# Eight more weight tiles per layer as three products, their rests by accumulating transfers, in a two-layer hybrid trunk

## The chip, the cores and the metric

The kernel runs on one core of a Trainium2 chip. The metric is the device time of one execution in microseconds (us), the median of several runs. Five engines work side by side, each in the order of its own queue: TensorE (PE: matrix products, with PEld for its weight loads), VectorE (DVE), ScalarE (ACT), GpSimd (POOL) and SyncE (SP). SP, ACT and POOL also issue transfers, which 16 DMA engines carry.

## The reference, cut to what matters

Two layers run over 272 tokens (16 learned ones and 256 of the input) of width 1024. Each layer is a mixer (a causal convolution and an attention, both gated) followed by a sparse part (PEER) that selects 16 of 16384 experts for each of 8 heads.

```python
def _mixer_block(x, ...):
    h = _rmsnorm(x, mix_g)
    z = h @ w_in
    conv_in, c_q, c_kv, k_rope, gate_logits = (z[..., :o0], z[..., o0:o1], z[..., o1:o2],
                                              z[..., o2:o3], z[..., o3:])
    ...
    gates = jax.nn.sigmoid(gate_logits)
    merged = gates[..., :D_MODEL] * y_conv + gates[..., D_MODEL:] * y_mla
    return x + merged @ w_out

def _peer(h, wq, keys, u_table, v_table):
    q = (hf @ wq).reshape(T, PEER_HEADS, 2, PEER_HALF)
    s = jnp.einsum('thpd,hpnd->thpn', q, keys)
    sv, si = lax.top_k(s, PEER_TOPK)
    ...
        a = jnp.einsum('ted,td->te', u_table[ib], xb)
        act = jax.nn.gelu(a) * wb
        return jnp.einsum('te,ted->td', act, v_table[ib])
```

The change touches two of the products: the gate logits (2048 columns of `w_in`, that is 16 tiles of 128) and the queries `hf @ wq` (2048 columns, 16 tiles).

## The kernel before, in words

The weights stream through a ring of four buffers of 1 MB (`wraw`); each holds two tiles of 128 x 1024. `next_w` takes the next tile and issues, on SP, the load that is due; `peek_w(n)` looks at the tile n further on. A load waits until the last reader of the buffer it overwrites is done.

A **plain tile** (`ztile`) is eight products of a 128 x 128 block of float32 weights with the activations (272 columns, in the second layer 256). Each shows in the profile as two matmul records, so a plain tile shows as x16. A **three-product tile** (`three`) splits weights and activations into a high part, rounded to the type float32r, and a rest: high x high, rest x high and high x rest, 24 products, each one record. `high` writes the high part of the weights (ACT), `low` the rest (weights less high part): on DVE, on POOL, or, for the query tiles 21, 23, 25 and 27, in two steps: ACT writes the negative of the weights (L711), and an accumulating transfer that POOL issues (L717) adds the weights: the destination holds the negative of the rounded weights, and w is added.

In the tables the key `"g5"` is gate tile 5, the keys 16 to 31 are the query tiles 0 to 15 (in the query loop the index is `16 + i`), and 0 to 15 are the output tiles between them. `kinds` gives the pair of buffers that a split uses: `wq0` and `wq1`, `seln` and `upad`, `acc` and `sqa`, halves of `kh` or of `sq`, or `wq0`/`wq1` with a part of `xh`.

One layer runs in this order on PE. First the tiles for queries, keys and the conv (four pairs, c = 0 to 3). Then the loop over 16 gate tiles (L859), each followed by a step of the attention (`next(att)`: key scales, scores, transposes, mixing) and by taps of the depthwise conv (`taps`: DVE multiplies and adds; `conv2` has ACT make products `cp`, which POOL's accumulating transfers sum into `part`, L673). Gate tiles 10 to 15 (`TPG`) are three-product tiles. Then the output products, and the loop over 16 query tiles (L1156): tiles 0 to 11 by three products, 12 to 15 plain. Each query tile is evacuated by ACT (`qr`, L1172); its scores against the keys are multiplied one tile later (`scores`), and DVE finds the best 16 (`top16`). Then the stage A multiplies all tokens with the table u (128 tiles), and a stage V with the table v, beside gathers of single expert rows.

Nine loads of u are issued early, inside the query loop: `EPLACE` gives, for the iteration that issues a load, which of the list `EARLY` it is and the buffer (`sq`, `kh`, `g0`, `g1`, or one of a pool of its own, `we`). Nothing reorders the program: each engine executes its instructions in the order in which the code issues them, and waits by semaphores. SP executes its loads in order too, so a load that waits holds back those behind it.

`MIXQ` names the tiles that live to the end of the query loop (pool `mpa`); the others of the mixer are in `mpb`, which is closed when the query loop begins (L982).

## Time and profile before

| | |
|---|---|
| median of 3 runs | 1658.9 us (1658.65 to 1661.19) |
| the profiled execution | 1659.62 us, its span 1657.8 us |
| mean granted TensorE clock | 1.000 |
| data moved | 568.52 MB, mean 343 GB/s |
| transfers of SP and ACT (q1), share of 16 engines | 50.7% |
| transfers of POOL (q0), share of 16 engines | 35.0% |

The profile is one execution. A group's line gives busy time and mean length; a timeline row gives start, length, engine, source line, operation, output and inputs, shapes and count, and in brackets the idle time before it and what ended it. A wait costs something only on the engine that sets the end at that place. Lengths of neighbouring matmuls overlap, so a tile is measured here from start to start. Lines are those of the kernel before.

### The profile page before, as it was taken

The page shows a single profiled execution, that of the slowest core. Times are in us where ns is not written, and L with a number is a line of the kernel's source. Part 1 is how long each engine was busy: PE and PEld are TensorE (multiplying, and loading weights), DVE is VectorE, ACT ScalarE, POOL GpSimd, SP SyncE. Part 2 cuts the span into 40 slices and gives each one's busy share as a digit, 9 for nine tenths or more (in the row PEclk, how much of TensorE's full clock was granted, in tenths as well). Part 3 has the DMA queues.
Part 4 walks back from the last instruction along what each step waited for, and adds up shares of the span by engine and source line. Part 5 has one row for each costly group of instructions (what it writes and reads, how often), then busy time and mean ns, then how long its engine had stood idle before and what let it go on. Part 6 is the DMA issues. An engine that isn't in the chain of part 4 may idle for free.

```text
span 1657.8 us, 30712 instructions
## 1 busy us (share of the span) xinstructions
PE 1642.4 (99%) x11827; PEld 1468.5 (89%) x11827; DVE 1261.6 (76%) x3082; ACT 693.3 (42%) x1803; POOL 333.0 (20%) x347
## 2 busy tenths in 40 slices
PE   9999999999999999999999999999999999999999
PEld 7679999999999999999986899999999997566655
DVE  5799899897898544444447998897877886788885
ACT  3565733435554111000024576433445443455554
POOL 0000033221222222222200100432211222233330
PEclk9999999999999999999999999999999999999999
DMA  6444697999999999999962746989999999999994
GB/s 249 113 128 177 242 345 298 424 383 424 416 423 418 424 424 423 424 424 424 417 259 85 176 153 242 340 348 396 362 425 409 409 391 411 420 425 425 424 425 191
DMA packets 86099, 568.52 MB, mean 343 GB/s; under 512 B 10328, under 2 KB 15384, under 8 KB 18744
## 3 DMA queue, kind: packets, MB, share of 16 engines
q1 hardware_dynamic: 50608, 338.51, 50.7%
q0 software_dynamic: 34560, 227.31, 35.0%
q8 instruction: 93, 1.52, 0.4%
q10 hardware_dynamic: 784, 0.74, 0.1%
q14 instruction: 54, 0.44, 0.1%
HBM read 556.18 MB, written 1.05 MB: 336 GB/s over the span
## 4 chain that ended last, share of the span: by engine, by line
PE 87%; DMA 8%; DVE 3%; ACT 1%; issue 1%; POOL 0%; SPq 0%; DVEq 0%; ACTq 0%; POOLq 0%
PE A L62 34%; PE po L62 25%; PE z L62 20%; DMA wraw<-vt 5%; PE aps L62 5%; PE wp L62 2%; DMA X<-vt 2%; DMA sqa<-wraw 1%; DVE acc L661 1%; PE xp L62 0%; PE sc L62 0%; DVE xh L1549 0%; PE wp L1262 0%; DVE tkw L1008 0%; ACT wr L1547 0%
## 5 line engine op out<-in xcount | busy, mean ns | idle before, releaser
L62 PE MATMUL A<-xh,wraw 128*128 128x160 f32 x3520 | 498.0, 300 | 0.0
L62 PEld LDWEIGHTS A<-xh,wraw 128*128 128x128 f32 x3520 | 481.1, 190 | 0.0
L62 PE MATMUL z<-xg,wraw 128*128 128x272 f32 (+2 forms) x832 | 194.1, 392 | 0.0
L1440 DVE SCALAR_TENSOR_TENSOR g<-g,xr 128x1024 f32<-128x1024 f32 x94 | 114.8, 1221 | 90.8 <-DMA g<-uv,iww 90.8
L62 PEld LDWEIGHTS z<-xg,wraw 128*128 128x128 f32 (+1 forms) x832 | 151.8, 189 | 35.0 <-issue 5.8
L1415 POOL DMA_INDIRECT g<-uv,iww x94 | 113.6, 1209 | 306.3 <-DVE va L1425 197.4
L1451 ACT ACTIVATE am<-am 128x1 f32<-128x1 f32 x208 | 40.9, 196 | 312.1 <-DVE g L1440 157.8
L62 PE MATMUL po<-Xh,wraw 128*128 128x160 f32 x1040 | 143.1, 300 | 1.0 <-DMA wraw<-vt 0.9
L62 PEld LDWEIGHTS po<-Xh,wraw 128*128 128x128 f32 x1040 | 141.5, 190 | 2.0 <-DMA wraw<-vt 2.0
L62 PE MATMUL po<-X,wraw 128*128 128x160 f32 x1008 | 138.4, 299 | 1.8 <-DMA wraw<-vt 1.3
L62 PEld LDWEIGHTS po<-X,wraw 128*128 128x128 f32 x1008 | 137.1, 190 | 2.7 <-DMA wraw<-vt 1.0
L1425 DVE SCALAR_TENSOR_TENSOR va<-g,am,va 128x1024 f32<-128x1024 f32 x91 | 116.5, 1281 | 0.3 <-ACT am L1452 0.2
L1340 ACT ACTIVATE ohA<-ohE,wlo 128x128 f16<-128x128 f16 x320 | 105.3, 428 | 5.2 <-DVE ohE L1337 4.4
L1440 DVE SCALAR_TENSOR_TENSOR kh<-kh,xr 128x1024 f32<-128x1024 f32 x48 | 58.6, 1221 | 42.5 <-DMA kh<-uv,iww 42.5
L1440 DVE SCALAR_TENSOR_TENSOR sq<-sq,xr 128x1024 f32<-128x1024 f32 x48 | 58.7, 1222 | 39.4 <-DMA sq<-uv,iww 39.4
L1415 POOL DMA_INDIRECT sq<-uv,iww x48 | 58.0, 1209 | 151.1 <-DVE va L1425 90.6
L1415 POOL DMA_INDIRECT kh<-uv,iww x48 | 59.9, 1248 | 140.4 <-DVE va L1425 92.8
L661 DVE SCALAR_TENSOR_TENSOR acc<-upad,cols,acc 128x272 f32<-128x272 f32 (+1 forms) x198 | 83.0, 485 | 0.2
L1351 ACT ACTIVATE Xh<-wp 128x260 f32<-128x260 f32 (+19 forms) x80 | 24.6, 307 | 131.5 <-DVE Xh L1348 124.8
L1425 DVE SCALAR_TENSOR_TENSOR va<-sq,am,va 128x1024 f32<-128x1024 f32 x48 | 61.5, 1281 | 5.5 <-ACT am L1452 5.5
L1425 DVE SCALAR_TENSOR_TENSOR va<-kh,am,va 128x1024 f32<-128x1024 f32 x48 | 61.5, 1282 | 3.7 <-ACT am L1452 3.7
L1452 ACT ACTIVATE am<-am,iww 128x1 f32<-128x1 f32 x208 | 61.3, 295 | 6.9
(503 smaller groups left out, 3075.0 us busy)
## 6 DMA issues: line engine op xcount, KB each, us to landing
wraw<-u SPq DMA_DIRECT2D x110, 1024.0 KB, 9.2
wraw<-vt SPq DMA_DIRECT2D x109, 1024.0 KB, 12.2
wraw<-w_in SPq DMA_DIRECT2D x27, 1024.0 KB, 4.7
X<-vt SPq DMA_DIRECT2D x17, 1024.0 KB, 11.4
wraw<-wq SPq DMA_DIRECT2D x16, 1024.0 KB, 4.8
we<-u SPq DMA_DIRECT2D x10, 1024.0 KB, 12.1
wraw<-w_out SPq DMA_DIRECT2D x8, 1024.0 KB, 4.6
wraw<-w_mla SPq DMA_DIRECT2D x4, 1024.0 KB, 5.1
```

Source lines behind the costliest of these rows:

```text
L62: PE.matmul(o, l, r, start=start, stop=stop, skip_group_check=True)
L661: V.scalar_tensor_tensor(acc[:, c, t0:], u_, weight(c, k), acc[:, c, t0:], op0=OP.mult, op1=OP.add)
L1340: S.activation(A_[1][:, t // 2, :, t % 2], E[0][:, t // 2, :, t % 2], AF.Copy, scale=wlo[:, 4 * b + t:4 * b + t + 1])
L1351: S.activation(x_, p[:, :, a:b].rearrange("p t j -> p j t"), AF.Copy, scale=1.0 / WS)
L1415: G.indirect_dma_start(out=g_, out_offset=None, in_=a[f"uv{l}"], in_offset=bass.IndirectOffsetOnAxis(ap=iww[i].bitcast(I32)[:, m // 16, 0, ...
L1425: V.scalar_tensor_tensor(vac[i], r, m_, vac[i], op0=OP.mult, op1=OP.add)
L1440: V.scalar_tensor_tensor(u_, u_, 1.0, xrs[i], op0=OP.mult, op1=OP.mult, accum_out=m_)
L1451: S.activation(m_, m_, AF.Gelu_apprx_tanh)
L1452: S.activation(m_, m_, AF.Copy, scale=iww[i][:, m // 16, 1, m % 16:m % 16 + 1])
```

## The change

Gate tiles 1, 3, 5 and 7 and query tiles 12 to 15 become three-product tiles, in both layers. Their rests, like those of query tiles 5, 7, 9 and 11 before, are made by an accumulating transfer (`BYDMA`). For all twelve the order of the products changes: high x high for the whole tile, then high x rest of the activations, and the rest of the weights last. Gate tiles 1 and 5 use `wq0` and `wq1`, tiles 3 and 7 a new buffer `gp`. The splits of tiles 1 and 3 are issued after the last conv pair, that of tile 5 after gate tile 1, that of tile 7 after gate tile 3. The splits of query tiles 12 to 15 are issued in the iterations 9 to 12. Since they hold `sq` and the activations' parts in `g0` and `g1` longer, three early loads of u move: `sq` from iteration 9 to 13, `g0` and `g1` from 12 and 13 to 15. Six names that only the query loop uses go to a pool of their own, opened when `mpb` is closed.

```diff
-TPG = (10, 11, 12, 13, 14, 15)
+TPG = (1, 3, 5, 7, 10, 11, 12, 13, 14, 15)
+ONLYQ = {"tkw0", "tkw1", "tkw2", "tkm", "scs", "qm"}
...
-EPLACE = {1: (4, None), 4: (0, "kh"), 5: (5, None), 7: (6, None), 8: (7, None), 9: (1, "sq"), 11: (8, None), 12: (2, "g0"), 13: (3, "g1")}
+EPLACE = {1: (4, None), 4: (0, "kh"), 5: (5, None), 7: (6, None), 8: (7, None), 11: (8, None), 13: (1, "sq"), 15: (2, "g0"), 15.5: (3, "g1")}
+BYDMA = ("g1", "g3", "g5", "g7", 21, 23, 25, 27, 28, 29, 30, 31)
...
-        kinds = {"g10": 0, "g11": 1, "g12": "k", "g13": 0, "g14": 1, "g15": "s", 0: "k", 1: 0, 2: 1, 3: "s", 4: "k",
-                 19: "k", 20: "a", 21: "q", 22: "w", 23: "s", 24: "q", 25: "a", 26: "s", 27: "w"}
+        kinds = {"g1": "v", "g3": "p", "g5": "v", "g7": "p", "g10": 0, "g11": 1, "g12": "k", "g13": 0, "g14": 1, "g15": "s", 0: "k", 1: 0, 2: 1, 3: "s", 4: "k",
+                 19: "k", 20: "a", 21: "q", 22: "w", 23: "s", 24: "q", 25: "a", 26: "s", 27: "w", 28: "q", 29: "a", 30: "s", 31: "w"}
...
-            if x == "w":
+            if x == "p":
+                t_ = mp.tile([128, 2048], F32, name="gp")
+                hi, lo = t_[:, 0:1024], t_[:, 1024:2048]
+            elif x in ("w", "v"):
                 hi, lo = [mp.tile([128, 1024], F32, name=f"wq{y}") for y in range(2)]
...
-            if i in (21, 23, 25, 27):
+            if i in BYDMA:
                 S.activation(parts[i][1], w_, AF.Copy, scale=-1.0)
...
             hi, lo, _ = parts[i]
+            if i in BYDMA:
+                for w_, x, f, e in ((hi, xs[0], first, None), (hi, xs[1], None, None), (lo, xs[0], None, end)):
+                    for c in cs:
+                        mm(p, w_[:, c * 128:(c + 1) * 128], x[:, c, t0:], c == f, c == e)
+                return
...
             next(att, None)
+            if c == 3:
+                for k in (1, 3):
+                    high(f"g{k}", k)
+                    low(f"g{k}")
...
-            new = [f"g{i + 2}"] if i + 2 in TPG else []
+            new = [f"g{i + 2}"] if i >= 8 and i + 2 in TPG else []
...
+            if i in (1, 3):
+                high(f"g{i + 4}", 3)
+                low(f"g{i + 4}")
...
         mixb.close()
+        qo.append(mixs.enter_context(tc.tile_pool(name=f"qo{l}", bufs=1)))
...
-            for k in {0: (2, 3), 1: (5,), 2: (4,), 3: (7,), 4: (6,), 5: (9,), 6: (8,), 7: (11,), 8: (10,)}.get(i, ()):
+            for k in {0: (2, 3), 1: (5,), 2: (4,), 3: (7,), 4: (6,), 5: (9,), 6: (8,), 7: (11,), 8: (10,), 9: (12,),
+                      10: (13,), 11: (14,), 12: (15,)}.get(i, ()):
```

Three places show how the order of instructions moves. ACT before, in layer 0, from the end of the conv pairs to the evacuation of gate tile 1 (`cp` are the conv copies, `g` the gates):

```order
L670 ACTIVATE cp<-upad,cols_61 128x272 x4
L832 ACTIVATE bz<-z 128x272
L459 ACTIVATE mq<-aps 128x272
L670 ACTIVATE cp<-upad,cols_61 128x272 x4
L874 ACTIVATE g_618<-z 128x272
L670 ACTIVATE cp<-upad,cols_61 128x272
L874 ACTIVATE g_618<-z 128x272
```

The same place on ACT now:

```order
L462 ACTIVATE mq<-aps 128x272
L673 ACTIVATE cp<-upad,cols_61 128x272 x4
L715 ACTIVATE wq_618<-wraw 128x1024
L717 ACTIVATE wq_619<-wraw 128x1024
L715 ACTIVATE gp<-wraw 128x1024
L717 ACTIVATE gp<-wraw 128x1024
L889 ACTIVATE g_627<-z 128x272
L673 ACTIVATE cp<-upad,cols_61 128x272
L889 ACTIVATE g_627<-z 128x272
L715 ACTIVATE wq_686<-wraw 128x1024
L717 ACTIVATE wq_687<-wraw 128x1024
```

Four copies of gate tiles 1 and 3 stand between the conv copies and the evacuation of gate tile 0; two of tile 5 follow the evacuation of tile 1.

PE now, in layer 0, from gate tile 0 to gate tile 3 (`seln` rows are the key scales, `kh,xh` rows the scores):

```order
L64 MATMUL z<-xg,wraw 128x272 x8
L64 MATMUL aps<-mq,seln 128x272 x4
L64 MATMUL z<-uk,wq_618 128x272 x8
L64 MATMUL z<-un,wq_618 128x272 x8
L64 MATMUL z<-uk,wq_619 128x272 x8
L64 MATMUL aps<-mq,seln 128x272 x4
L64 MATMUL aps<-kh,xh 128x144
```

Before, one plain tile (`z<-xg,wraw`, x8) stood in the place of the three rows between the key scales; now the rest of the weights (`wq_619`) is read by the last eight of 24 products, one plain tile and four small products after gate tile 0 began.

SP before, in layer 0, at the end of the query loop (`iww` is the spread of the selected indices, which waits for DVE):

```order
L1170 DMA sq<-u 128x2048
L95 DMA wraw<-u 128x2048
L1170 DMA we_2619<-u 128x2048
L95 DMA wraw<-u 128x2048
L1170 DMA g_2669<-u 128x2048
L1170 DMA g_2717<-u 128x2048
L95 DMA wraw<-u 128x2048
L1150 DMA iww_1975<-ew 128x1x64
```

The same place on SP now:

```order
L97 DMA wraw<-u 128x2048
L1191 DMA we_2716<-u 128x2048
L97 DMA wraw<-u 128x2048
L1191 DMA sq<-u 128x2048
L97 DMA wraw<-u 128x2048
L1169 DMA iww_2060<-ew 128x1x64
L1191 DMA g_2939<-u 128x2048
L1191 DMA g_2941<-u 128x2048
```

The load into `sq` stands behind two ring loads and one early load that it preceded, the loads into `g0` and `g1` behind a ring load and the spread of the indices.

More of the change, by code (lines that the diff above doesn't have):

```diff
@@ L34 @@
 EARLY = (0, 1, 2, 3, 8, 10, 12, 14, 16)
-EPLACE = {1: (4, None), 4: (0, "kh"), 5: (5, None), 7: (6, None), 8: (7, None), 9: (1, "sq"), 11: (8, None), 12: (2, "g0"), 13: (3, "g1")}
+EPLACE = {1: (4, None), 4: (0, "kh"), 5: (5, None), 7: (6, None), 8: (7, None), 11: (8, None), 13: (1, "sq"), 15: (2, "g0"), 15.5: (3, "g1")}
+BYDMA = ("g1", "g3", "g5", "g7", 21, 23, 25, 27, 28, 29, 30, 31)
 JS = 63
-MIXQ = {"xg", "uk", "qr", "rq_w", "rq_x", "rq_ym", "tkw0", "tkw1", "tkw2", "tkm", "sk", "scs", "qm",
+MIXQ = {"xg", "uk", "qr", "rq_w", "rq_x", "rq_ym", "sk",
         "wq0", "wq1", "seln", "upad", "acc", "sqa", "g0", "g1"}
@@ L230, in trunk_kernel @@
         mixb = ExitStack()
+        qo = []
         mpa = mixs.enter_context(tc.tile_pool(name=f"mixq{l}", bufs=1))
@@ L237, in tile @@
             def tile(shape, dt, name, **kw):
-                return (tw if name in ("sq", "kh", "g0", "g1") else mpa if name in MIXQ else mpb).tile(shape, dt, name=name, **kw)
+                return (tw if name in ("sq", "kh", "g0", "g1") else qo[0] if name in ONLYQ else mpa if name in MIXQ else mpb).tile(shape, dt, name=name, **kw)
         zs = ExitStack()
@@ L715, in low @@
             hi, lo, w_ = parts[i]
-            if i in (21, 23, 25, 27):
+            if i in BYDMA:
                 G.dma_start(lo, w_, accum_op=OP.add)
@@ L723, in three @@
             hi, lo, _ = parts[i]
+            if i in BYDMA:
+                for w_, x, f, e in ((hi, xs[0], first, None), (hi, xs[1], None, None), (lo, xs[0], None, end)):
+                    for c in cs:
+                        mm(p, w_[:, c * 128:(c + 1) * 128], x[:, c, t0:], c == f, c == e)
+                return
             for c in cs:
@@ L1162, in trunk_kernel @@
                 z = ztile(t0)
-            for k in {0: (2, 3), 1: (5,), 2: (4,), 3: (7,), 4: (6,), 5: (9,), 6: (8,), 7: (11,), 8: (10,)}.get(i, ()):
+            for k in {0: (2, 3), 1: (5,), 2: (4,), 3: (7,), 4: (6,), 5: (9,), 6: (8,), 7: (11,), 8: (10,), 9: (12,),
+                      10: (13,), 11: (14,), 12: (15,)}.get(i, ()):
                 high(16 + k, k - i - 1)
                 low(16 + k)
-            if i in EPLACE:
-                k, n = early_[l][EPLACE[i][0]], EPLACE[i][1]
-                raws[k] = (two(n).rearrange("p (a b) -> p a b", a=2) if n else
-                           ep.tile([128, 2, 1024], F32, name=f"we{i}"))
-                nc.sync.dma_start(raws[k], srcs[k])
+            for e in (i, i + 0.5):
+                if e in EPLACE:
+                    k, n = early_[l][EPLACE[e][0]], EPLACE[e][1]
+                    raws[k] = (two(n).rearrange("p (a b) -> p a b", a=2) if n else
+                               ep.tile([128, 2, 1024], F32, name=f"we{i}"))
+                    nc.sync.dma_start(raws[k], srcs[k])
             qT_ = mp.tile([128, T], F32, name="qr", bufs=2)
```

## The prediction, made before the changed kernel ran

> **What bounds the kernel now.** The first part of the page gives each engine's busy time, share of the span and instruction count. The fourth gives the chain that ended last.
>
> ```profile
> PE 1642.4 (99%) x11827; PEld 1468.5 (89%) x11827; DVE 1261.6 (76%) x3082; ACT 693.3 (42%) x1803; POOL 333.0 (20%) x347
> ...
> PE 87%; DMA 8%; DVE 3%; ACT 1%; issue 1%; POOL 0%; SPq 0%; DVEq 0%; ACTq 0%; POOLq 0%
> ```
>
> TensorE (PE) is the bound, but 99% is an average over stages. The change touches two stages per layer: the gate tiles (60 to 145 us in layer 0) and the query tiles (198 to 257 us). The view by stretches shows both; its columns are stretch, length, busy time of PE, weight loads, DVE, ACT and POOL, the granted clock, DMA share and GB/s.
>
> ```profile
> 80.00:120.00 40.00, 40.00 (x234) 31.72 (x227) 36.15 (x100) 26.51 (x76) 2.57 (x3) 1.00 0.52 146
> 200.00:240.00 40.00, 40.00 (x326) 39.05 (x325) 35.76 (x230) 19.20 (x36) 19.04 (x16) 1.00 0.93 307
> ```
>
> PE has no idle time in either, so a shorter tile pays at once and a new wait of PE costs in full. DVE is close behind at 36 of 40 us. The view of waits says how little PE waits now:
>
> ```profile
> PE z L62 <- DMA sqa<-wraw: 1.7, 1, 1.7
> ...
> PE aps L62 <- DVE zkr L747: 0.7, 1, 0.7
> ```
>
> The first row matters: in layer 1 PE already waited 1.7 us for a rest made by an accumulating transfer, the device that the change uses in twelve tiles per layer instead of four.
>
> **What a tile gains.** The timeline of PE (start, length, instruction) around one three-product tile (x24) and one plain tile (x16) of layer 0, and score starts around one of each in layer 1:
>
> ```profile
> 234.26 0.61 PE L62 MATMUL sc<-uk,qr 128*128 128x128 f32 x4
> 234.62 3.26 PE L62 MATMUL z<-g,wq 128*128 128x272 f32 x24
> 237.72 0.61 PE L62 MATMUL sc<-uk,qr 128*128 128x128 f32 x4
> 238.16 3.83 PE L62 MATMUL z<-xg,wraw 128*128 128x272 f32 x16
> 241.83 0.61 PE L62 MATMUL sc<-uk,qr 128*128 128x128 f32 x4
> ...
> 1047.12 0.61 PE L62 MATMUL sc<-uk,qr 128*128 128x128 f32 x4
> 1050.40 0.60 PE L62 MATMUL sc<-uk,qr 128*128 128x128 f32 x4
> ...
> 1072.83 0.61 PE L62 MATMUL sc<-uk,qr 128*128 128x128 f32 x4
> 1076.72 0.61 PE L62 MATMUL sc<-uk,qr 128*128 128x128 f32 x4
> ```
>
> From score to score a plain tile takes 241.83 - 237.72 = 4.11 us, a three-product tile 237.72 - 234.26 = 3.46: a gain of 0.65 us. In layer 1 (256 columns) it is 3.89 - 3.28 = 0.61. Eight tiles per layer: 8 x 0.65 + 8 x 0.61 = 10.1 us, if nothing waits.
>
> **Gate tile 1: a new wait.** Its two copies and its transfer are issued only after the conv copies of ACT at the end of the last pair, one plain tile ahead of their use. The rows of ACT and PE at that place, layer 0 and layer 1:
>
> ```profile
> 71.58 1.75 ACT L670 ACTIVATE cp<-upad,cols 128x272 f32<-128x272 f32 x4
> 75.72 3.93 PE L62 MATMUL z<-xg,wraw 128*128 128x272 f32 x16
> ...
> 911.60 1.85 ACT L670 ACTIVATE cp<-upad,cols 128x256 f32<-128x256 f32 x4
> 915.52 3.72 PE L62 MATMUL z<-xg,wraw 128*128 128x256 f32 x16
> ```
>
> The price of making a rest this way is seen at query tile 5 (21 in the tables): two copies, POOL's issue, and the landing counted from that issue (then the spread over all eight such transfers, and the quickest one of the conv's partial sums, 408 KB instead of 512).
>
> ```profile
> 199.28 1.05 ACT L709 ACTIVATE sq<-wraw 128x1024 fp32r<-128x1024 f32 x1
> 200.23 1.05 ACT L711 ACTIVATE sq<-wraw 128x1024 fp32r<-128x1024 f32 x1
> 201.81 0.86 POOL L717 DMA_DIRECT2D sq<-wraw  x1 [92.12 <-PE z L62]
> ...
> DMA to landing us min/median/max: 6.2/6.2/6.2
> ...
> DMA to landing us min/median/max: 6.2/9.1/12.6
> ...
> DMA to landing us min/median/max: 4.1/4.1/4.1
> ```
>
> So: conv copies end at 73.33, two copies take 0.95 + 1.05 = 2.0, POOL starts 0.53 later: issued at 75.86. With the undisturbed 6.2 us the rest lands at 82.1. The changed tile runs its 16 products with the high part first, 16/24 of 3.10 us, so PE reaches the rest at 75.72 + 2.07 = 77.8 and **waits 4.3 us**. Layer 1: issued at 911.60 + 1.85 + 2.0 + 0.53 = 915.98, landed at 922.2, needed at 915.52 + 1.93 = 917.45: **4.7 us**. Queued behind it on PE are the key scales, all scores and every later gate tile, and DVE waits for those. I take 6.2 because weights are nearly loaded there; by 4.1 the waits are 2.2 and 2.6, by 12.6 they are 10.7 and 11.1. Below nothing they can't be: even the quickest landing misses by 2 us.
>
> [...]
>
> Tiles 3, 5 and 7 are issued two tiles or more ahead, some 10 us, and wait for nothing at 6.2. The eight copies on ACT (8.4 us) lie in its idle time before the first softmax; the evacuation of tile 0 comes 4 us later, covered by three buffers. Without that cover it would cost PE those 4 us. POOL's later conv transfers queue behind the rests but are wanted only at 118 us.
>
> Gates: 4.3 - 4 x 0.65 = +1.7 in layer 0, 4.7 - 4 x 0.61 = +2.3 in layer 1. DVE is pushed back by the wait too and catches up in its own idle time:
>
> ```profile
> 112.43 1.36 DVE L492 TENSOR_REDUCE mx<-aps 128x1 f32<-128x144 f32 x4 [1.55 <-PE aps L62]
> ```
>
> That swallows 1.55 us; the rest is late at the layer norm, where PE waits already in layer 1. I add 0.3 (between 0 and 1).
>
> **The last four query tiles.** They gain 4 x 0.65 = 2.6 and 4 x 0.61 = 2.4. Their copies stand on ACT behind a wide copy that itself waits for DVE:
>
> ```profile
> 230.96 1.91 ACT L1064 ACTIVATE tx<-it 128x2048 f16<-128x2048 f16 x1 [3.71 <-DVE it L1062]
> ...
> 1060.59 1.91 ACT L1064 ACTIVATE tx<-it 128x2048 f16<-128x2048 f16 x1 [2.99 <-DVE it L1062]
> ...
> 1073.73 0.35 ACT L1083 ACTIVATE ew<-ce,rsT 128x64 f32<-128x64 f32 x1 [2.86 <-DVE ce L1082]
> ```
>
> In layer 0 the copies of the first of the four (tile 12) run from 232.8 to 234.8, so the evacuation behind them ends at 235.1 and the score that PE had at 234.26 waits 0.8. The rest is issued at 235.3, lands at 241.5 and is needed at 238.16 + 0.8 + 2.07 = 241.0: 0.5 more. With 10 us, as a neighbour's transfer had, it would be 4. The next three are ahead. Layer 0: -2.6 + 1.3 = -1.3.
>
> In layer 1 the same gives 0.9 and 0.6, and the last tile, whose copies stand behind the copy at 1073.73, about 1.0 (0.4 to 1.8). The old wait of 1.7 goes, because the rest is now used last. Layer 1: -2.4 - 1.7 + 2.5 = -1.6. Without any new wait the two layers would give -6.7.
>
> **Loads that move.** Three loads of u go later on SP, two of them behind the spread of the indices:
>
> ```profile
> 255.31 0.62 SPq L1150 DMA_DIRECT2D iww<-ew  x1
> ...
> 257.09 4.61 PE L62 MATMUL A<-xh,kh 128*128 128x160 f32 x32 [0.59 <-ACT idxT L1036]
> ...
> 266.76 8.45 PE L62 MATMUL A<-xh,g 128*128 128x160 f32 x61
> ...
> 256.00:260.00 4.00, 3.41 (x31) 3.06 (x30) 3.96 (x28) 1.01 (x4) 0.00 (x0) 1.00 0.04 8
> ```
>
> They can start at about 256 and are wanted at 265.5 and 4.5 us later. The DMA engines are idle there (0.04), so two loads of 1 MB have 9 us. I cost them at nothing; behind other traffic they took this long:
>
> ```profile
> DMA to landing us min/median/max: 14.8/15.9/16.8
> ```
>
> and then PE would wait 256 + 15.9 - 265.4 = 6.5 us per layer. The pool for query-only tiles issues nothing; its first writes come long after the last use of the memory under it: nothing.
>
> **Sum:** 1.7 + 2.3 + 0.3 - 1.3 - 1.6 = **+1.4 us**. The profiled execution took 1659.6 us (span 1657.8), so 1661.0 for it; the median of the runs is 0.7 lower: **1660.3 us**, 0.1% above before. A measurement of this kernel can tell about 0.2% (3.3 us) from no change.
>
> **Rivals.**
> - *The rests land early* (4.1 us): gates 2.2 + 2.6 - 5.0 = -0.2, queries -6.7 + 1.7 = -5.0: 1653.7. For it: less weight traffic at the gates. Against it: none of eight landed under 6.2. Chance 0.15.
> - *PE comes back slow.* [...] Its first products, at the start of the program, show the slow rate: 22 in 5.06 us is 0.23 us each, against 0.11 for a score product (0.44 for 4):
>
> ```profile
> 2.01 5.06 PE L62 MATMUL z<-ones 128*128 128x128 f32 x22 [2.01 <-DVE strip L144]
> ```
>
>   Half of 5 us is lost, 2.5 per layer: 1665.3. It decides only if the wait is long enough; no later wait in this trace passes 2 us, so no row shows the threshold. Chance 0.12. [...]
> - *The rests queue behind weights* (9.1 us, the median above): 2.9 more at tile 1 and at the first of the four query tiles, in both layers: +11.6, 1671.9. For it: seven of eight were slower than 6.2. Against it: three loads of u leave just that stretch of the query tiles. Chance 0.13.
> - *The moved loads are late*: 13 us, 1673.3. Chance 0.05.
> - *DVE is the true bound of the query stage*, and its savings don't arrive: +4.3, 1663.2. DVE is full from 228 to 256, but its last results are copied away by ACT for PE. Chance 0.07.
>
> My case holds 0.48, of which 0.43 lies within 0.2% and 0.05 above. Faster by over 0.2%: 0.15 (the first rival). Slower by over 0.2%: 0.05 + 0.12 + 0.13 + 0.05 + 0.07 = 0.42. The range from 1653.5 to 1666 leaves out the two rivals near 1672 (0.18).
>
> **What would show it.** In the trace after, PE should wait once per layer at gate tile 1 for `wq<-wraw`, 4 to 5 us; gate tiles 3, 5 and 7 not at all; the first query tile of the four under 1 us; the wait for `sqa<-wraw` in layer 1 gone; the A stage without a wait for `g<-u`. Gate wait under 2.5 us, or two waits of over 2 us among the queries, would make the prediction wrong. So would products of 0.23 us behind the wait.

## The result and the profile after

The changed kernel takes 1677.0 us (median of four runs, 1675.5 to 1678.0) beside 1659.1 us for the kernel before on the same chip: a ratio of 1.0105, interval 1.0087 to 1.0122. The change costs 18 us. 1660.3 was predicted, between 1653.5 and 1666; the measured time lies 11 us above that range. The profiled execution has a span of 1674.2 us, 16.4 more than before, and its mean granted clock is 0.993, not 1.000.

The first row of the page's part 1, and the first row of its chain, for the kernel after:

```profile
PE 1643.3 (98%) x11955; PEld 1474.3 (88%) x11955; DVE 1262.3 (75%) x3082; ACT 722.9 (43%) x1835; POOL 364.5 (22%) x363
...
PE 86%; DMA 9%; DVE 2%; issue 1%; ACT 1%; POOL 0%; DVEq 0%; SPq 0%; POOLq 0%; ACTq 0%
```

PE has almost the same busy time as before (1642.4), though eight tiles per layer should need 10 us less. So PE lost time in two ways: it stood idle 15 us more, and it was slower while busy. The view of PE's waits names the idle part (engine and tile, what it waited for: total us, times, longest):

```profile
PE z L64 <- DMA sq<-wraw: 7.8, 2, 4.4
PE z L64 <- DMA wq<-wraw: 7.6, 3, 3.3
...
PE sc L64 <- ACT qr L1193: 1.2, 2, 0.7
...
PE aps L64 <- DVE zkr L758: 0.7, 1, 0.7
PE z L64 <- DMA upad<-wraw: 0.5, 1, 0.5
PE z L64 <- DMA sqa<-wraw: 0.2, 1, 0.2
```

The new rows add up to 17.3 us (7.8 + 7.6 + 1.2 + 0.5 + 0.2), less the 1.7 us of the old wait for `sqa`: 15.6. The five that matter, in PE's timeline: gate tile 1 of layer 0 with what follows it, then query tile 12 of layer 0, gate tile 1 of layer 1, query tiles 12 and 15 of layer 1. (The names show which buffer a product reads: `z<-uk,wq x8` behind `z<-un,wq` are the rest products of gate tile 1.)

```profile
75.37 1.28 PE L64 MATMUL z<-uk,wq 128*128 128x272 f32 x8
76.48 1.16 PE L64 MATMUL z<-un,wq 128*128 128x272 f32 x8
80.95 1.27 PE L64 MATMUL z<-uk,wq 128*128 128x272 f32 x8 [3.31 <-DMA wq<-wraw]
82.16 1.29 PE L64 MATMUL aps<-mq,seln 2*128 2x272 f32 x8
83.38 3.14 PE L64 MATMUL aps<-kh,xh 98*128 98x144 f32 x8
86.31 5.14 PE L64 MATMUL z<-xg,wraw 128*128 128x272 f32 x16
...
248.55 1.52 PE L64 MATMUL z<-g,sq 128*128 128x272 f32 x8 [3.45 <-DMA sq<-wraw]
...
928.25 1.78 PE L64 MATMUL z<-uk,wq 128*128 128x256 f32 x8 [2.73 <-DMA wq<-wraw]
...
1086.18 2.08 PE L64 MATMUL z<-g,sq 128*128 128x256 f32 x8 [4.38 <-DMA sq<-wraw]
...
1100.30 1.21 PE L64 MATMUL z<-g,wq 128*128 128x256 f32 x8 [1.50 <-DMA wq<-wraw]
```

Read the lengths behind the first wait: the eight products for the key scales take 1.29 us (0.74 before), the scores 3.14 (1.67), the plain tile 5.14 (3.93). The view by stretches has the reason in its clock column (stretch, length, busy time of PE, weight loads, DVE, ACT, POOL, the granted clock, DMA share, GB/s):

```profile
80.00:82.00 2.00, 1.04 (x8) 1.05 (x8) 0.00 (x0) 0.00 (x0) 0.00 (x0) 1.00 0.96 184
82.00:84.00 2.00, 2.00 (x12) 1.15 (x12) 0.54 (x2) 1.74 (x3) 0.00 (x0) 0.53 0.91 287
84.00:86.00 2.00, 2.00 (x7) 1.65 (x7) 2.00 (x6) 2.00 (x3) 1.16 (x2) 0.50 0.58 246
86.00:88.00 2.00, 2.00 (x6) 1.54 (x5) 1.97 (x8) 0.71 (x4) 0.59 (x1) 0.50 1.01 195
88.00:90.00 2.00, 2.00 (x8) 1.53 (x8) 2.00 (x6) 2.00 (x9) 0.00 (x0) 0.76 1.04 198
```

From 82 to 89 us TensorE had half its clock. What that costs is 2 us times the part missing in each row: 2 x (0.47 + 0.50 + 0.50 + 0.24) = 3.4 us, as much as the wait itself. The same sum gives 3.4 us behind the wait of gate tile 1 in layer 1 and 1.7 behind each wait of query tile 12.

To see where the 16.4 us arise, take five stretches of the program, each from one PE instruction to the next: the **gate stretch** from the first key-scale product (75.04 us before) to the first query score (201.63), the **query stretch** from there to the first product of A (257.09), the **long stretch** of both tables to the first key-scale product of layer 1 (914.85), and gate and query stretch of layer 1 (to 1034.05 and 1086.47). After, they are longer by 4.2, 3.4, 0.5, 3.7 and 5.2 us; the start and the end of the program, outside the five, are 0.8 us shorter together. Four of them agree with the parts read above: wait + clock - gain is 3.3 + 3.4 - 2.6 = 4.1 and 2.7 + 3.4 - 2.4 = 3.7 for the gates; 4.2 + 1.7 - 2.6 = 3.3 for the queries of layer 0, and 7.1 - 1.7 + 1.7 - 2.4 = 4.7 for those of layer 1, half a microsecond short. These sums are my reading; the experiments test them.

### The profile page after: what moved, and what is told of

Same layout as the page of the kernel before. It is cut to its first block, busy times and chain, and to the rows that moved or that the text cites. A ratio compares the mean times of both kernels' runs of the same rounds, so it can differ in the third digit from the quotient of the medians.

```text
span 1674.2 us, 31059 instructions
## 1 busy us (share of the span) xinstructions
PE 1643.3 (98%) x11955; PEld 1474.3 (88%) x11955; DVE 1262.3 (75%) x3082; ACT 722.9 (43%) x1835; POOL 364.5 (22%) x363
## 3 DMA queue, kind: packets, MB, share of 16 engines
q0 software_dynamic: 36864, 235.70, 37.1%
HBM read 556.18 MB, written 1.05 MB: 333 GB/s over the span
## 4 chain that ended last, share of the span: by engine, by line
PE 86%; DMA 9%; DVE 2%; issue 1%; ACT 1%; POOL 0%; DVEq 0%; SPq 0%; POOLq 0%; ACTq 0%
PE A L64 33%; PE po L64 25%; PE z L64 18%; DMA wraw<-vt 5%; PE aps L64 5%; PE wp L64 2%; DMA wq<-wraw 1%; DMA X<-vt 1%; DVE acc L664 1%; DMA sq<-wraw 1%; PE sc L64 1%; PE xp L64 0%; DVE xh L1570 0%; PE wp L1283 0%; ACT wr L1568 0%
## 5 line engine op out<-in xcount | busy, mean ns | idle before, releaser
L1436 POOL DMA_INDIRECT g<-uv,iww x94 | 123.7, 1316 | 297.6 <-DVE va L1446 196.9
L64 PE MATMUL z<-xg,wraw 128*128 128x272 f32 (+2 forms) x576 | 135.8, 398 | 0.0
L64 PEld LDWEIGHTS z<-xg,wraw 128*128 128x128 f32 (+1 forms) x576 | 105.7, 190 | 27.5 <-issue 5.1
```

Source lines behind the costliest of these rows:

```text
L64: PE.matmul(o, l, r, start=start, stop=stop, skip_group_check=True)
L1436: G.indirect_dma_start(out=g_, out_offset=None, in_=a[f"uv{l}"], in_offset=bass.IndirectOffsetOnAxis(ap=iww[i].bitcast(I32)[:, m // 16, 0, ...
```

## The experiments

Fifteen kernels. The table has what each stretch took beyond the kernel before in its profiled execution, in us, and the timed result. Each entry is one execution: pool_q_g357 and pool_q_g357_l0, whose code is the same up to the gates of layer 1, differ by 1.2 us in the long stretch. The start and the end of the program, which have no column, add between -0.9 and +2.7 us.

| kernel | gates, layer 0 | queries, layer 0 | long | gates, layer 1 | queries, layer 1 | median us | ratio to before, interval |
|---|---|---|---|---|---|---|---|
| after | +4.2 | +3.4 | +0.5 | +3.7 | +5.2 | 1677.0 | 1.0087 to 1.0122 |
| gates_only | +4.1 | -0.1 | +0.2 | +9.8 | -2.0 | 1673.0 | 1.0050 to 1.0098 |
| queries_only | 0.0 | +4.5 | 0.0 | 0.0 | +4.6 | 1668.1 | 1.0035 to 1.0068 |
| order_loads | 0.0 | -0.1 | +1.4 | 0.0 | -2.0 | 1658.1 | 0.9976 to 0.9995 |
| filled | +0.7 | +2.6 | +0.3 | +2.7 | +5.8 | 1673.1 | 1.0068 to 1.0102 |
| part_filled | +0.7 | +1.9 | +0.4 | +6.0 | +5.3 | 1675.8 | 1.0076 to 1.0120 |
| early_rests | +4.0 | +2.1 | +0.3 | +2.1 | +4.2 | 1673.7 | 1.0071 to 1.0115 |
| queries_less_load | 0.0 | +3.2 | +2.4 | +0.1 | +2.5 | 1666.5 | 1.0024 to 1.0050 |
| pool_gate1 | -0.7 | +3.4 | +2.0 | +1.0 | +5.5 | 1675.3 | 1.0082 to 1.0119 |
| pool_all | +0.9 | -2.1 | +3.8 | +5.4 | -3.2 | 1665.2 | 1.0019 to 1.0045 |
| pool_queries | 0.0 | -2.1 | +4.3 | 0.0 | -3.2 | 1658.4 | 0.9984 to 1.0002 |
| pool_q_g357 | -2.0 | -2.0 | +2.4 | +3.5 | -3.2 | 1659.5 | 0.9989 to 1.0007 |
| pool_q_g57 | -1.3 | -2.0 | +2.8 | +3.6 | -3.2 | 1660.5 | 0.9995 to 1.0013 |
| pool_q_g357_kd | -2.0 | -2.0 | +3.2 | +8.4 | -3.2 | 1664.0 | 1.0013 to 1.0031 |
| pool_q_g357_l0 | -2.0 | -2.0 | +3.6 | 0.0 | -3.2 | 1657.1 | 0.9969 to 0.9988 |
| l0_sq9 | -2.0 | -2.0 | +1.9 | 0.0 | -3.2 | 1656.6 | 0.9974 to 0.9992 |

### Which part loses it

gates_only makes the last four query tiles plain again:

```diff
-8: (10,), 9: (12,), 10: (13,), 11: (14,), 12: (15,)}.get(i, ())
+8: (10,)}.get(i, ())
```

> The changed kernel with its last four query tiles plain again; gate tiles 1, 3, 5 and 7 keep three products. Theory A (the time is lost where PE waits for a late rest, and half as much again because the granted clock then stands near 0.5 for some 6 us): gate tile 1 costs the waits of 3.3 and 2.7 us plus 3.4 us of clock in each layer, the four tiles gain 5.0, and the product order gains 1.7: 1659.1 + 6.0 + 6.8 - 5.0 - 1.7 = 1665.2. Theory B (the waits are all, and the lower clock has another cause, such as more work per us on the engines): 1659.1 + 6.0 - 5.0 - 1.7 = 1658.4 with the clock at 1.00 in the query stage and possibly at the gates. Theory C (the gates are innocent, the queries lose it all): 1653.

queries_only makes gate tiles 1, 3, 5 and 7 plain again:

```diff
-TPG = (1, 3, 5, 7, 10, 11, 12, 13, 14, 15)
+TPG = (10, 11, 12, 13, 14, 15)
-                for k in (1, 3):
+                for k in ():
-            if i in (1, 3):
+            if i in ():
```

> The changed kernel with gate tiles 1, 3, 5 and 7 plain again; the last four query tiles keep three products. Theory A: new waits of 4.2 us in layer 0 and 7.1 in layer 1, 3.5 us of clock, less 5.0 for the tiles and 1.7 for the old wait: 1659.1 + 8.1 = 1667.2. Theory B (the waits alone): 1663.7. If the gates lose it all: 1653 or less.

order_loads has both edits.

> What is left of the change without any new three-product tile: rest products last in query tiles 5, 7, 9 and 11, three loads of u later, query-only tiles in their own pool. Theory A: the old wait for sqa in layer 1 goes, nothing else: 1659.1 - 1.7 = 1657.4. Rival (the moved loads or the pool cost something by themselves): 1659 or more, with PE waiting for g in the stage after the query tiles.

Measured: 1673.0, 1668.1 and 1658.1. Both parts lose, and what is left without them is 0.1% faster than before (0.9976 to 0.9995): 2.0 us are gained in the query stretch of layer 1, where the old wait for `sqa` is gone, and 1.4 us lost in the long stretch. queries_only came out as theory A said; order_loads is near its 1657.4, though the loss in the long stretch was not in that theory. gates_only did not: its gate stretch in layer 1 is 9.8 us longer, not 3.7. The wait for the rest is 3.6 us there, and a second one has come, at the layer norm, which theory A did not have. PE's waits in gates_only, and then DVE's from 905 to 1000 us:

```profile
PE aps L64 <- DVE zkr L758: 3.6, 1, 3.6
```

```profile
DVE acc L682 <- DMA part<-cp: 2.9, 1, 2.9
```

PE waits for DVE's sum `zkr`, and DVE has waited for the conv's last partial sum, which a transfer of POOL's queue adds up. That is the same queue in which the rests now stand. This is taken up below.

### Is it the idle time that halves the clock?

filled gives PE more work: products whose sums are thrown away, ahead of the real ones, of about the length of the wait.

```diff
+FILL = {'g1': (25, 21), 28: (27, 36)}
...
             if i in BYDMA:
+                for y in range(FILL[i][l] if i in FILL else 0):
+                    mm(p, hi[:, y % 8 * 128:y % 8 * 128 + 128], xs[0][:, y % 8, t0:], True, True)
                 for w_, x, f, e in ((hi, xs[0], first, None), (hi, xs[1], None, None), (lo, xs[0], None, end)):
```

> The changed kernel with more work: ahead of the real products of gate tile 1 and query tile 12, PE runs 25 and 27 (layer 0), 21 and 36 (layer 1) extra products, whose sums are thrown away, so that it arrives at the rest about when the rest lands. Theory A (the clock halves because PE stood idle): the rests come as late as before, the waits shrink to under 1 us, the granted clock stays at 1.00 there, and the time falls by the 10 us of clock: 1677 - 10.3 = 1666.7. Theory B (the clock falls for another reason): no gain, 1677 or more, with the clock still at 0.5 behind both places.

part_filled is the same with `{'g1': (10, 14), 28: (15, 16)}`.

> The changed kernel with fewer extra products ahead of gate tile 1 (10 in layer 0, 14 in layer 1) and query tile 12 (15 and 16), so that waits of about 2.0, 1.0, 1.5 and 2.5 us remain. If the clock falls after any wait, it falls after all four. If it takes an idle window as long as the shortest wait that was followed by a fall so far (2.7 us), the granted clock stays at 1.00 behind all four and the time is near 1673, as with all waits filled. If the threshold lies between, the windows behind each wait show where.

The mean clock of filled is 1.000 in the profiled execution (0.997 to 1.000 in all four), and with more work the kernel is no slower but rather faster: its span is 5.1 us shorter than that of the kernel after, its median 3.9 (the intervals of the two ratios overlap). At gate tile 1 of layer 0 the reading is exact. PE's timeline of filled there, the same place as above, and then the rest products of query tiles 13, 14 and 15 of layer 1:

```profile
75.34 4.41 PE L65 MATMUL z<-uk,wq 128*128 128x272 f32 x33
79.58 1.16 PE L65 MATMUL z<-un,wq 128*128 128x272 f32 x8
80.68 1.27 PE L65 MATMUL z<-uk,wq 128*128 128x272 f32 x8
81.88 0.74 PE L65 MATMUL aps<-mq,seln 2*128 2x272 f32 x8
...
84.06 3.83 PE L65 MATMUL z<-xg,wraw 128*128 128x272 f32 x16
...
1085.72 1.20 PE L65 MATMUL z<-g,sqa 128*128 128x256 f32 x8 [1.51 <-DMA sqa<-wraw]
...
1090.27 1.22 PE L65 MATMUL z<-g,upad 128*128 128x256 f32 x8 [1.03 <-DMA upad<-wraw]
...
1095.24 1.21 PE L65 MATMUL z<-g,wq 128*128 128x256 f32 x8 [1.41 <-DMA wq<-wraw]
```

The rest is used as late as before (80.68 against 80.95), but what follows runs at 0.74 and 3.83 instead of 1.29 and 5.14, and the gate stretch shrinks from +4.2 to +0.7, the 3.4 us of clock. So theory A holds for the cause. It fails on the size: 10.3 us were expected, 3.9 came. At the gates of layer 1 only 1.0 us was won, because PE waited 1.6 us for ACT and 1.1 for `zkr` later in that stretch. In the query stretch of layer 1 nothing was won (+5.8), though the clock is 1.00. The last rows say why: the rests of tiles 13, 14 and 15 come 4.6 to 5.0 us apart whatever PE does, and a faster PE only waits for them longer. There the lost clock had been hidden behind the next late rest.

part_filled leaves shorter waits. The rest products of gate tile 1 in layer 0 and a plain tile behind, then query tile 12 of layer 1 and the layer norm's product before it, in its timeline:

```profile
81.09 1.26 PE L65 MATMUL z<-uk,wq 128*128 128x272 f32 x8 [1.78 <-DMA wq<-wraw]
...
84.47 3.83 PE L65 MATMUL z<-xg,wraw 128*128 128x272 f32 x16
...
977.07 1.19 PE L65 MATMUL aps<-zkr,ones 128*128 128x256 f32 x2 [3.31 <-DVE zkr L761]
...
1084.05 1.73 PE L65 MATMUL z<-g,sq 128*128 128x256 f32 x8 [2.90 <-DMA sq<-wraw]
```

Behind the waits of 1.78, 1.56 and 1.08 us the clock is 1.00 in every stretch of 2 us; behind 2.90 it is 0.62 and 0.52, and around the end of the 3.31 us for `zkr` 0.50 for some 6 us. In queries_less_load a wait of 2.18 us left the clock at 1.00, and one of 2.44 was followed by half clock.

The length of a wait alone doesn't decide, however. pool_gate1 and pool_all (described below) have the same code at the gates, and in layer 0 both wait 1.55 us for DVE just ahead of a plain tile. The rows of pool_gate1, then of pool_all:

```profile
81.81 0.97 PE L65 MATMUL aps<-kh,xh 98*128 98x144 f32 x4 [1.55 <-DVE kh L473]
82.62 3.83 PE L65 MATMUL z<-xg,wraw 128*128 128x272 f32 x16
...
81.97 0.97 PE L65 MATMUL aps<-kh,xh 98*128 98x144 f32 x4 [1.55 <-DVE kh L473]
82.78 5.52 PE L65 MATMUL z<-xg,wraw 128*128 128x272 f32 x16
```

Behind the same wait the tile takes 3.83 us in one and 5.52 in the other. In layer 1 it is the other way round: both wait 1.45 us for DVE, and it is pool_gate1 whose clock then halves. The clock as the traces record it shows part of the reason. Within a run, all falls lie multiples of 3.41 us apart (in the kernel after at 82.12, 249.37, 928.63 and 1085.64 us, which is 49, 199 and 46 such steps), half clock lasts one step or two, 3.41 or 6.83 us, and the steps lie differently against the program in each run. Counted over all runs, every step at full clock in which PE stood idle for more than 1.9 us was followed by half clock, none with less than 1.1 us of idle time was, and between the two some were. The 1.55 us lie in one step in pool_all (79.50 to 82.91) and across two in pool_gate1 (which meet at 80.47); the 1.45 us lie in one step in both kernels, so the place of the steps is not all of it, and the rest stays open. In these runs, then, every wait of 2.44 us or more at full clock was followed by half clock, at a price of up to 1.7 or 3.4 us, and of the waits between 1.4 and 2.2 us two were.

### Why the rests of the query tiles are late

early_rests issues the copies and transfers of tiles 12 to 15 one tile earlier:

```diff
-8: (10,), 9: (12,), 10: (13,), 11: (14,), 12: (15,)}
+8: (10, 12), 9: (13,), 10: (14,), 11: (15,)}
```

> The changed kernel with the copies and transfers of query tiles 12 to 15 issued one tile earlier each (tile 12's together with tile 10's). Theory A1 (the rest of tile 12 is late because ACT and POOL issue it late): it lands before its use, the waits of 3.5 and 4.4 us and the clock behind them go, and the time falls by the 3.4 + 5.3 us that the stage lost and the 2.3 + 2.4 it should gain: some 13, to 1664. Theory A2 (the DMA engines are full there from 226 to 258 us, and four more rests of about 2.6 us of all 16 engines each don't fit, whenever they are issued): the waits move to tiles 13 to 15 or to the loads behind them, and the time falls by less than 6 us, to 1671 or more.

queries_less_load is queries_only with two early loads moved behind query tile 15 (and named by their number, so that both have a buffer):

```diff
-7: (6, None), 8: (7, None), 11: (8, None), 13: (1, "sq"), 15: (2, "g0"), 15.5: (3, "g1")}
+7: (6, None), 13: (1, "sq"), 15: (2, "g0"), 15.5: (3, "g1"), 15.6: (7, None), 15.7: (8, None)}
```

> The kernel with plain gate tiles and transfers for query tiles 12 to 15 (queries_only, 1668.1), with two of the 1 MB loads of u moved from query tiles 8 and 11 to behind tile 15; no other edit. Theory A2 (the rests queue behind loads on full DMA engines): the rest of tile 12 lands up to 3 us sooner in each layer, the waits for sq fall under 2.5 us, the clock stays at 1.00, and the time falls by 5 to 9 us, to 1659 to 1663. Theory A1 (issued too late, the loads don't matter): landing times as before, 9 to 10 us from POOL's issue, and 1668.

In the kernel after, POOL's issue of tile 12's rest in both layers, from the timeline; and from the view by stretches the DMA share (the column before the last) while it is on its way in layer 0:

```profile
239.12 0.88 POOL L723 DMA_DIRECT2D sq<-wraw  x1 [7.40 <-issue]
...
1076.14 0.88 POOL L723 DMA_DIRECT2D sq<-wraw  x1 [6.14 <-issue]
```

```profile
244.00:248.00 4.00, 1.10 (x9) 0.88 (x7) 3.81 (x25) 2.49 (x4) 1.33 (x2) 1.00 1.05 273
248.00:252.00 4.00, 3.45 (x22) 2.84 (x23) 1.07 (x6) 1.03 (x3) 0.88 (x1) 0.67 1.07 214
```

The rest is used 9.4 us after its issue (248.55 - 239.12) and 10.0 in layer 1. All 16 DMA engines are busy (share 1.07), and yet move 214 GB/s, where the kernel before, with no rest on its way, moved 424 at a share of 1.01 (244 to 248 us, the row is shown below). At 424 GB/s a load of 512 KB would take them 1.2 us, an estimate; a rest takes longer. From the shares of POOL's queue (37.1% of 1674.2 us with sixteen more rests than pool_queries, below, 34.7% of 1658.3) an estimate is (621.1 - 575.4) / 16 = 2.9 us of all 16 engines for each; beside the kernel before (35.0% of 1657.8 us, as many rests as pool_queries) it is 2.6.

early_rests came to 1673.7, where theory A2 had 1671 or more. Tile 12 no longer waits, but tiles 14 and 15 wait 1.7 and 1.3 us in layer 0, and tile 14 waits 2.8 in layer 1, where a score also waits 1.8 us for ACT, which now makes the copies earlier: the wait has moved. queries_less_load shows the other side. Tile 12's rest and those products of tile 15 that wait for theirs, in both layers:

```profile
235.27 0.88 POOL L723 DMA_DIRECT2D sq<-wraw  x1 [7.41 <-issue]
...
242.04 1.27 PE L64 MATMUL z<-g,sq 128*128 128x272 f32 x8 [0.79 <-DMA sq<-wraw]
...
256.09 1.27 PE L64 MATMUL z<-g,wq 128*128 128x272 f32 x8 [2.90 <-DMA wq<-wraw]
...
1090.61 2.08 PE L64 MATMUL z<-g,wq 128*128 128x256 f32 x8 [2.44 <-DMA wq<-wraw]
```

Without the two loads the rest takes 6.8 us (9.7 in queries_only: issued at 235.01, used at 244.66), and in layer 1 7.8 instead of 10.7. So the rests do queue behind loads, as A2 says. The median fell by 1.6 us and not by 5 to 9: the wait went on to tile 15, whose rest takes 11 us. Four rests and the loads do not fit into that stretch in any order tried.

### The rests from POOL instead

pool_gate1 has the rest of gate tile 1 made by a subtraction on POOL, products still in the new order; pool_all does so for query tiles 12 to 15 too.

```diff
-BYDMA = ("g1", "g3", "g5", "g7", 21, 23, 25, 27, 28, 29, 30, 31)
+BYDMA = ('g3', 'g5', 'g7', 21, 23, 25, 27)
+BYPOOL = ('g1', 28, 29, 30, 31)
...
-                (G if i in (20, 22, 24, 26) else V).tensor_tensor(lo, w_, hi.bitcast(F32), op=OP.subtract)
+                (G if i in (20, 22, 24, 26) or i in BYPOOL else V).tensor_tensor(lo, w_, hi.bitcast(F32), op=OP.subtract)
```

> The changed kernel with the rest of gate tile 1 made by POOL (a subtraction of 2.4 us, as in query tiles 4, 6, 8 and 10) instead of by an accumulating transfer, everything else as changed. Theory A (the wait for that one rest and the clock behind it are all that the gate stage loses): no wait at gate tile 1, the clock at 1.00 there, and the stage gains its 2.6 and 2.4 us: 1677 - 6.8 - 6.1 = 1664. Rival (three products at gates 3, 5 and 7 or the copies on ACT cost something too): 1667 or more, with new waits of PE in the gate stage.

> The changed kernel with the rests of gate tile 1 and of query tiles 12 to 15 made by POOL; gates 3, 5 and 7 keep the transfer. Theory A2 (full DMA engines): the twelve accumulating transfers of 2.6 us that are gone from the crowded stretch leave room, no wait of PE over 1 us in either stage, and the eight tiles gain their 10.1 us and the 1.7 of the old wait: 1647 to 1650. Rival (DVE is the bound of the query stage, or DVE and POOL slow each other): 1654 or more, with DVE busy all through the last query tiles and the waits of PE on DVE or ACT instead of on a transfer.

In the query stretches pool_all gives what was hoped for: -2.1 and -3.2 us, no wait for a transfer, and waits of 0.4 and 1.0 us for DVE, which is close behind. At the gates POOL is a poor place. The wait for the rest is gone, but in layer 0 only 0.7 of the 2.6 us are won, and layer 1 loses 1.0, with 1.7 us of half clock behind its wait of 1.45 us. DVE and POOL of pool_gate1 in layer 1, and then the same five taps of DVE in order_loads, where POOL does not subtract:

```profile
917.50 4.45 DVE L665 SCALAR_TENSOR_TENSOR acc<-upad,cols,acc 128x256 f32<-128x256 f32 x5
...
918.83 2.44 POOL L726 TENSOR_TENSOR wq<-wraw,wq 128x1024 fp32r<-128x1024 f32 x1
```

```profile
914.32 2.32 DVE L664 SCALAR_TENSOR_TENSOR acc<-upad,cols,acc 128x256 f32<-128x256 f32 x5
```

Five conv taps take 4.45 us instead of 2.32 while POOL subtracts for 2.44: DVE takes 2.1 us longer over them, and PE then waits 1.55 us for DVE's scaled keys (layer 0, the row at 81.81 shown above). That the two come together is measured; why the taps take longer is not shown.

pool_all came to 1665.2, not 1647 to 1650 (ten transfers are gone in it, five per layer, not twelve as expected). Its misses are the gate stretch of layer 1 (+5.4, with 3.6 us of waiting for `zkr`; the same gate code lost only 1.0 in pool_gate1, where that wait was 0.7), that of layer 0 (+0.9, where pool_gate1 gained 0.7: the 1.7 us of half clock shown above) and the long stretch (+3.8).

### Which gains are kept

pool_queries, pool_q_g357 and pool_q_g57 have POOL's rests in query tiles 12 to 15 and, of the gates, none, tiles 3, 5 and 7, or tiles 5 and 7 by transfers.

> The changed kernel with all gate tiles 1, 3, 5 and 7 plain again and the rests of query tiles 12 to 15 made by POOL. Theory (in the query stage only the transfers are wrong; three products there are worth their price if the rest comes from an engine that is idle): the query stage gains 2.1 us in layer 0 and 3.2 in layer 1, as its stretches did with all rests on POOL, the gate stage is as before: 1659 - 5 = 1654. Rival (that gain was made only because the gate stage ahead had put DVE late or early): 1657 or more.

> As pool_queries, with gate tiles 3, 5 and 7 as three products by transfers (tile 1 plain). Theory A as it stood before the runs (only tile 1's rest is late): 3 x 0.65 + 3 x 0.61 = 3.8 us faster than pool_queries, 1650. Theory D (DVE is the bound of the gate stage in layer 1, and conv's partial sums, which DVE adds, queue behind the rests): layer 0 gains about 1.9, layer 1 nothing or loses up to 3.5 at the layer norm, where PE waits for zkr: 1652 to 1656.

> As pool_q_g357 without tile 3, whose transfer is issued between conv's partial sums. Theory D: the partial sums land in time, the wait for zkr in layer 1 is back at 0.7 us, and two tiles per layer gain up to 2.5 us: 1652 to 1654, no worse than with tile 3. If the partial sums are not it, the wait for zkr stays at 3 us or more.

pool_queries keeps -2.1 and -3.2 in the query stretches, as expected, and yet measures 1658.4, the same as before: 4.3 us come back in the long stretch and 1.4 at the start and the end of the program. In pool_q_g357, gates 3, 5 and 7 gain their full 3 x 0.65 = 2.0 us in layer 0 without any wait, and lose 3.5 in layer 1. PE's wait at the layer norm, and then DVE's from 905 to 985 us:

```profile
PE aps L65 <- DVE zkr L759: 3.0, 1, 3.0
```

```profile
DVE acc L683 <- DMA part<-cp: 2.0, 1, 2.0
```

That is gates_only again without tile 1. Leaving out tile 3 as well (pool_q_g57) did not help: 3.6 us for `zkr`. My guess that it was the transfer of tile 3 between the partial sums was wrong. The next two look at the layer norm of layer 1 from two sides. pool_q_g357_l0 keeps gates 3, 5 and 7 in layer 0 only; pool_q_g357_kd takes one of the six partial sums off the queue in layer 1:

```diff
-            if i in TPG:
+            if i in TPG and (i >= 8 or l == 0):
-            if i in (1, 3):
+            if l == 0 and i in (1, 3):
```

> As pool_q_g357, but gate tiles 3, 5 and 7 are three products in layer 0 only; layer 1 has plain ones. Theory D (in layer 1 conv's partial sums, queued behind the rests, are late for the layer norm; in layer 0 nothing waits): the gate stage of layer 0 keeps its gain of 2.0 us, that of layer 1 is as before instead of 3.7 us longer, so 1659.5 - 3.7 = 1656, the stretches fed by memory taking back part of it. Rival (what the earlier stages save is always taken back by the loads of the long stage): 1658 to 1660, like pool_queries and pool_q_g357.

```diff
-            for k in range(0, KD, 3):
+            for k in range(0, (KD if l == 0 else KD - 3), 3):
```

> As pool_q_g357, with one of conv's six accumulated transfers of partial sums in layer 1 given back to DVE (three more taps of 0.41 us there). Theory D: the last partial sum lands some 7 us sooner, DVE no longer waits for it, PE's wait for zkr in layer 1 falls from 3.0 us to under 1.5, the clock stays at 1.00 behind it, and the gate stage of layer 1 is 3 us or more shorter: 1656. Rival (DVE's own work is the bound there): the wait for zkr stays or grows by up to 1.2 us, 1660 or more.

pool_q_g357_l0 is 1657.1 us, ratio 0.9979 (0.9969 to 0.9988): faster than before by 0.2%, with the gate stretch of layer 1 at 0.0 and the wait for `zkr` back at 0.7 us. POOL's last partial sum is issued 30.5 us after the first key-scale product in it (914.16 to 944.70) and 37.7 us after it in pool_q_g57 (914.16 to 951.83). In pool_q_g57 ACT's copy for the sum before the last stood 5.3 us until an earlier sum had landed, which no copy of pool_q_g357_l0 does at that place. So the rests do delay the partial sums, by some 7 us.

pool_q_g357_kd came to 1664.0: not theory D's 1656, and within the rival's 1660 or more, but not for the rival's reason. The wait for `zkr` went, but with fewer partial sums DVE's program adds them up earlier, in the midst of the softmax, and stands there:

```profile
950.68 1.34 DVE L683 TENSOR_TENSOR acc<-acc,part 128x256 f32<-128x256 f32 x3 [7.88 <-DMA part<-cp]
```

7.88 us for the transfer, not for its own work; PE then waits 3.9 us for the softmax, and the clock halves. It confirms what DVE waits for, not what an earlier sum would be worth.

### What the moved loads cost

l0_sq9 is pool_q_g357_l0 with the load into `sq` back at query tile 9, which other buffers for tiles 12 to 15 allow:

```diff
-13: (1, "sq"), 15: (2, "g0"), 15.5: (3, "g1")}
+9: (1, "sq"), 15: (2, "g0"), 15.5: (3, "g1")}
-28: "q", 29: "a", 30: "s", 31: "w"}
+28: "a", 29: "s", 30: "w", 31: "a"}
```

> As pool_q_g357_l0 (1657.1), with query tiles 12 to 15 using other free buffers, so that the 1 MB load into sq goes back from query tile 13 to tile 9. Theory L (the moved loads are owed later: the DMA engines stand idle before the A stage and are full behind it): the stretch from A to the gates of layer 1 gets shorter by about 1 MB at 420 GB/s, 2.5 us, from 3.6 over before to about 1, a little also in layer 1: 1654 to 1655. Rival (what starts earlier is taken back by the rate of the loads, wherever this one stands): the stretch stays 3 us or more over before, 1657.

The long stretch fell from +3.6 to +1.9, less than the 2.5 us expected but in that direction; the median is 1656.6, which the runs cannot tell from 1657.1. It doesn't show theory L. The stretch ahead of A, in the view by stretches, first of the kernel before, then of pool_q_g357_l0, last of l0_sq9:

```profile
244.00:248.00 4.00, 4.00 (x21) 3.41 (x20) 3.93 (x28) 0.83 (x4) 0.00 (x0) 1.00 1.01 424
248.00:252.00 4.00, 4.00 (x22) 3.38 (x21) 3.90 (x12) 0.83 (x4) 0.00 (x0) 1.00 0.76 299
```

```profile
244.00:248.00 4.00, 3.56 (x29) 3.38 (x29) 3.90 (x26) 0.85 (x4) 0.02 (x1) 1.00 0.43 174
248.00:252.00 4.00, 3.90 (x37) 3.53 (x36) 3.86 (x13) 1.01 (x6) 0.00 (x0) 1.00 0.00 0
...
244.00:248.00 4.00, 3.58 (x29) 3.40 (x28) 3.90 (x26) 0.89 (x4) 0.00 (x0) 1.00 0.03 12
```

Before, the loads run until 251 us. In pool_q_g357_l0 the loads into `g0` and `g1` are issued only at 256.85 us, and the DMA engines stand idle from about 246 on. But the load into `sq` was brought ahead of A there too. Put back to tile 9, it only lets the engines run dry earlier, from about 244 on: up to 252.8 us, where A starts, SP's and ACT's queue has moved 45.87 MB in both kernels, beside 48.00 MB up to A in the kernel before. So l0_sq9 brings no more ahead of A, and its 1.7 us have no shown cause; they are little more than the 1.2 us that pool_q_g357 and pool_q_g357_l0 differ by with the same code. That the two loads which are missing, 2.1 MB, are owed in the long stretch, where the engines are full (a share of 1.01 from 400 to 440 us in the kernel before, 1.00 in the kernel after), fits these numbers, but no run puts those two back.

## Why the prediction was wrong

**What bounds the kernel: right.** PE's idle time and its speed set the time; the five stretches, with the start and the end of the program, add up to the 16.4 us.

**What a tile gains: right.** 0.65 and 0.61 us: gates 3, 5 and 7 gained 2.0 us in layer 0. The query tiles gained 2.1 and, with the old wait's 1.7, 3.2 us where no rest was late, short of 2.6 and 4.1 by about the 0.4 and 1.0 us that PE then waits for DVE.

**Gate tile 1's wait: right in place, too large in size.** 4.3 and 4.7 us were predicted, 3.3 and 2.7 came; the rest took 5.8 and 4.8 us from issue to use, not 6.2. That alone would have made the change cheaper.

**What follows the wait: the first failure.** The sum let PE go on at full speed. The half clock stood among the rivals, as deciding only behind a wait that is long enough, with half of 5 us, once per layer, at a chance of 0.12. No row of the kernel before shows how long that is (its later waits stay under 2 us), and behind its own waits of 4.3 and 4.7 us the sum put the term at nothing. The only 5 us in a row are those of the program's first products (22 in 5.06 us); no run shows half clock of that length: it lasted 3.41 or 6.83 us. Half clock came behind waits of 2.7 to 4.4 us, four times, and cost 3.4 us behind the gates and 1.7 behind query tile 12. filled shows the cause. Why one wait is followed by one step of half clock and another by two is open.

**Query tile 12: the second failure.** The step said that the rest lands 6.2 us after its issue, and waits 0.5 us; it landed after 9.4 and 10.0, and PE waited 3.5 and 4.4. I took the quickest of the eight transfers seen instead of their median, because three loads leave that stretch. They did not help: the DMA engines were full (shares of 1.05 and 1.07 from 244 to 252 us), and four more rests of 2.6 to 2.9 us each filled them further. "The next three are ahead" failed too: in layer 1 tiles 13 to 15 waited 2.2 us together. The delays of the scores by ACT's copies (0.8 and 0.9) came as 0.7 and 0.5.

The rival "rests queue behind weights" (1671.9) had this mechanism, and the half clock is a second rival. I priced them as alternatives. They are one chain: the later a rest, the longer the wait, and a wait that is long enough costs clock as well. With the measured sizes the chain gives 15.6 of waits + 10.2 of clock - 10.1 of gain = 15.7 us, where the spans differ by 16.4.

**The partial sums at nothing: wrong, though not in the changed kernel.** "Wanted only at 118 us" was argued for layer 0, where it holds. In layer 1 PE waited 3.0 to 3.6 us at the layer norm in five of the kernels with rests at the gates. In the changed kernel, whose stages were late anyway, DVE did not wait for the partial sums, and PE's wait stayed at 0.7.

**The moved loads at nothing: right in the changed kernel, open beyond it.** No product of A waits for them there, as predicted; in pool_q_g357_l0, whose A starts earlier, one waits 0.9 us. The long stretch is 1.4 us longer in order_loads and up to 4.3 where the query stretch is short; in the changed kernel, whose query tiles end 7.3 us later, it is 0.5. How much of that is the price of the moved loads is not shown.

**The old wait gone: right.** -2.0 us in order_loads, predicted 1.7.

## What to carry to other kernels

A product that waits for its operand costs the wait and, when the wait is long enough, up to 1.7 or 3.4 us of clock on top (always from 2.4 us on in these runs, now and then from 1.45); so a gain of 0.6 us per tile is only worth having if the operand is there in time, and where it cannot be, throw-away products in the gap can keep the clock up at no cost, as in filled (mean clock 1.000 instead of 0.993, the span 5.1 us shorter). Before a transfer is given the work of an idle engine, look at the DMA share in that very stretch and take the median landing, not the quickest. When an early stage is made shorter, look at what the loads behind it were using the time for.

## What the hardware showed unexpectedly

- The granted clock changes in steps of 3.41 us: half clock lasted 3.41 or 6.83 us, and within a run the falls lie multiples of 3.41 us apart. It came with every PE wait of 2.44 us or more, and with two of the shorter ones (1.45 us in pool_gate1, 1.55 in pool_all), while waits of the same length in the other of these two kernels left the clock at 1.00. A fall can begin up to 2.1 us before PE resumes (gates_only, at 980.31 for a wait that ends at 982.37) or up to 2.3 us after (early_rests, at 928.76 after 926.49).
- An accumulating transfer of 512 KB inside SBUF takes 2.6 to 2.9 us of all 16 DMA engines (estimated above from the shares of POOL's queue), while loads from memory passed at 424 GB/s in the kernel before (244 to 248 us), by which 1 MB is estimated at 2.5 us.
- Five conv taps of DVE took 4.45 us beside a subtraction of 2.44 us on POOL (pool_gate1, layer 1), 2.1 more than the 2.32 us without one (order_loads); in the query tiles PE waits 0.4 and 1.0 us for DVE with such subtractions (pool_all), and whether they are the reason was not separated.
